# A two-layer encoder trunk on one core: from a planned order to the order of the text on every engine

## The chip, the core and the metric

The kernel runs on one core of a Trainium2 chip. TensorE (PE) multiplies; its weight loads (PEld) overlap its products. VectorE (DVE), ScalarE (ACT) and GpSimd (POOL) do the rest, SyncE (SP) issues most transfers. The metric is the device time of one execution in microseconds, median of the runs shown.

## The reference

The input is 256 tokens of 2048 features, and a memory of 256 tokens of 2048 features. Layer A normalises the tokens, multiplies by `a_w_in` (3584 columns), sends 1536 of them through a causal convolution and a gated linear recurrence (RG-LRU: sigmoid gates from 12 small products, then a scan over the tokens), gates the result by the GeLU of 1536 others, and lets the last 512 attend to the memory. Layer B has multi-head latent attention in place of the recurrence, and the same attention to the memory. Both layers end with `w_o` (2048 x 2048), a normalised residual, an MLP with squared ReLU (2048 to 8192 and back), and another normalised residual. Each layer makes memory keys and values from the normalised memory with weights of its own. All is float32.

## The kernel before, in words

Every weight block comes from DRAM as float32 and is split: ACT rounds it to float32r (`whi`, L108), DVE takes the rest (`wlo`, L109). `weights` (L116 to L131) loads 512 KB (two k-tiles of 512 columns) through SP's queue into one of five `wraw` buffers, and four `whi` and four `wlo` buffers hold what PE may use next. Activations are split in the same way into X tiles. `gemm` (L134 to L197) makes a block of columns: per k-tile and 128 outputs a 512-column and a 256-column product where features are wanted on partitions (L156, L157), or three products per 128 tokens where tokens are wanted on partitions (L166 to L168).

The order of each engine is planned: the framework simulates the program and issues by priority, with `tc.high_priority` around weight splits and evacuations. Work beside the products sits in generators (`bg`), a stage of which is traced after each group of k-tiles (`tick`), and the planner still moves it.

The stages in order, with the lines used below: memory values of layer A, whose X tiles grow from transposes of the memory (`to_features`, L231 to L252, transposes at L243); parameters (`rows`, L270 to L281, loaded through SP); tokens, their sums of squares (`stats`, L221) and transposes; memory keys; queries to the memory; three times a 512-column block of the recurrent branch and one of its gate (convolution L590 to L596, gates L599 to L606, recurrence L614 to L631 with a reciprocal at L623, GeLU L645 to L658, partly on POOL); `w_o` (`mix_out`); residual (`residual`, additions at L447); the MLP (8 blocks of two up and four down products); then layer B. The memory is transposed three times: once for layer A's keys and values, and once each for layer B's keys and values (`mem_features`, L528). The narrow last blocks of `PARTS` shorten the end of `mix_out` and of the MLP. The output leaves at L451.

Of the kernel before, what the change touches and what calls it, by code (L numbers as in the profile page):

```python
# [10 lines left out]
F32 = mybir.dt.float32  # L11
# [18 lines left out]
# columns of the output of a last block: narrow at the end, where the next phase waits for it  # L30
PARTS = [(0, 512), (512, 512), (1024, 512), (1536, 256), (1792, 256)]
SKEW = 1
# [15 lines left out]
def trunk(ctx: ExitStack, tc: tile.TileContext, a: dict, out: bass.AP):  # L48
# [16 lines left out]
    ctx.callback(phase.close)  # L65

# [1 line left out]
    # Work that fills the engines beside the products: generators, a stage of each running one per tick.  # L68
    # None in the queue: what follows waits for all before it.
# [3 lines left out]
    def tick():  # L73
# [7 lines left out]
        if bg:  # L81
            g = bg.popleft()
            if not next(g, True):
                active.append(g)
# [20 lines left out]
    def split(dst_hi, dst_lo, src, g=None):  # L105
        """dst_hi + dst_lo = src (times the column g), dst_hi rounded to float32r."""
# [9 lines left out]
    def weights(src, nk, n, gains=None):  # L116
        """[nk * 128, n] of DRAM, each row times its gain, as two float32r tiles [128, nk, n]."""
        raw = wp.tile([P, 1024], F32, name="wraw", tag="wraw", bufs=5)[:, : nk * n]
        nc.sync.dma_start(out=raw.rearrange("p (k n) -> p k n", k=nk), in_=src.rearrange("(k p) n -> p k n", p=P))
        hi = wp.tile([P, 1024], F32R, name="whi", tag="whi", bufs=4)[:, : nk * n]  # L120
        lo = wp.tile([P, 1024], F32R, name="wlo", tag="wlo", bufs=4)[:, : nk * n]
        with tc.high_priority(offset=200):
            if gains is None:
                split(hi, lo, raw)
            else:
                for k, g in enumerate(gains):
                    c = slice(k * n, (k + 1) * n)
                    split(hi[:, c], lo[:, c], raw[:, c], g)
        return hi.rearrange("p (k n) -> p k n", k=nk), lo.rearrange("p (k n) -> p k n", k=nk)
# [4 lines left out]
    def gemm(X, src, nk, n, bcols=(), a=None, evac_b=None, evac_a=None, kts=None, gain=None, pre=None, skew=0):  # L134
# [4 lines left out]
        kts = list(range(src.shape[0] // P)) if kts is None else kts  # L139
        groups = []  # L140
        for kt in kts:
            if groups and len(groups[-1]) < nk and groups[-1][-1] + 1 == kt:
                groups[-1].append(kt)
            else:
                groups.append([kt])
        W = {}
        psb = [mm.tile([P, 512], F32, name="psb", tag="mm") for _ in bcols]
        psa, one_bank = {}, False

        def by_features(i):  # L150
            ks, hi, lo = W[i]
            for j, b in enumerate(bcols):
                for k, kt in enumerate(ks):
                    Xk = X[kt // 4][:, kt % 4, :]
                    first, last = (i, k) == (0, 0), (i, k) == (len(groups) - 1, len(ks) - 1)
                    nc.tensor.matmul(psb[j], hi[:, k, b : b + P], Xk, start=first, stop=False)  # L156
                    nc.tensor.matmul(psb[j][:, 256:512], lo[:, k, b : b + P], Xk[:, 0:256], start=False, stop=last)  # L157

        def by_tokens(t, i):
            ks, hi, lo = W[i]  # L160
            for k, kt in enumerate(ks):
                Xk = X[kt // 4][:, kt % 4, :]
                xh, xl = Xk[:, t * P : (t + 1) * P], Xk[:, 256 + t * P : 256 + (t + 1) * P]
                first, last = (i, k) == (0, 0) and not (one_bank and t), (i, k) == (len(groups) - 1, len(ks) - 1)
# [4 lines left out]
                if last:  # L169
                    with tc.high_priority(offset=100):  # L170
                        evac_a(t, psa[t])

        for i, ks in enumerate(groups):
            if pre is not None:
                pre(ks[0])
            gains = gain and [gain(kt) for kt in ks]
            W[i] = (ks, *weights(src[ks[0] * P : (ks[-1] + 1) * P, :], len(ks), n, gains))
            if a is not None and i == 0:
                na = a(W[0][1][:, 0, :]).free_size()
                one_bank = na <= 256 and not skew  # L180
# [6 lines left out]
            if a is not None:  # L187
                by_tokens(0, i)
                if i >= skew:
                    by_tokens(1, i - skew)  # L190
            tick()
        if a is not None:
            for i in range(len(groups) - skew, len(groups)):
                by_tokens(1, i)
        with tc.high_priority(offset=100):
            for j in range(len(bcols)):
                evac_b(j, psb[j])  # L197
# [11 lines left out]
    def as_row(dst, r):  # L209
        """dst[p, token] = r of the token: [128, 256] from [128, 2]."""  # L210
# [12 lines left out]
    def rstd(dst, ss, n):  # L223
        """dst = (sum of ss over its last axis / n + EPS) ** -0.5, a column for every token block"""
# [6 lines left out]
    def to_features(chunk, nkt, gain, X, qs=None):  # L231
        """X (a list of X tiles) grows by the features of tokens, transposed, times gain(k), split.
        chunk(t, q): [128 tokens, up to 512 features] from feature 512 q."""
        for q in range(0, nkt, 4) if qs is None else [4 * q for q in qs]:
            kn = min(4, nkt - q)
            src = [chunk(t, q // 4) for t in range(NT)]
            X.append(xtile())
            for k0 in range(0, kn, 2):
                ps = aux()
                for k in range(k0, k0 + 2):  # L240
                    for t in range(NT):
                        c = (k - k0) * T + t * P
                        nc.tensor.transpose(ps[:, c : c + P], src[t][:, k * P : (k + 1) * P], ident)  # L243
                if gain is None:
                    split(X[-1][:, k0 : k0 + 2, 0:256], X[-1][:, k0 : k0 + 2, 256:512], ps.rearrange("p (k n) -> p k n", k=2))
                    continue
                for k in range(k0, k0 + 2):
                    c = (k - k0) * T
                    split(X[-1][:, k, 0:256], X[-1][:, k, 256:512], ps[:, c : c + T], gain(q + k))

    def scaled(src, r):
        """chunk() of tokens src [128, 2, n] scaled by the columns r."""  # L252

        def chunk(t, q):
            n = min(512, src.shape[2] - 512 * q)
            hn = scr(n, "hn")
# [635 lines left out]
```

## Time and profile before

| what | value |
|---|---|
| median of 3 runs | 2129.55 us (2128.59 to 2129.86) |
| profiled execution, first to last instruction (span) | 2126.1 us |
| PE busy | 2090.0 us, 98% |
| DVE, ACT, POOL busy | 1344.1, 1078.2, 99.1 us |
| DMA over the span | 394.98 MB, mean 186 GB/s |

The page gives the profiled execution its span; no total beside it is listed, and the median is 3.45 us more than the span. A busy PE is not PE at its peak, since matmul ends are modelled. Idle time of another engine costs only where PE waits for it.

### The profile page before, as it was taken

The page shows a single profiled execution, that of the slowest core. Times are in us where ns is not written, and L with a number is a line of the kernel's source. Part 1 is how long each engine was busy: PE and PEld are TensorE (multiplying, and loading weights), DVE is VectorE, ACT ScalarE, POOL GpSimd, SP SyncE. Part 2 cuts the span into 40 slices and gives each one's busy share as a digit, 9 for nine tenths or more (in the row PEclk, how much of TensorE's full clock was granted, in tenths as well). Part 3 has the DMA queues.
Part 4 walks back from the last instruction along what each step waited for, and adds up shares of the span by engine and source line. Part 5 has one row for each costly group of instructions (what it writes and reads, how often), then busy time and mean ns, then how long its engine had stood idle before and what let it go on. Part 6 is the DMA issues. An engine that isn't in the chain of part 4 may idle for free.

```text
span 2126.1 us, 29360 instructions
## 1 busy us (share of the span) xinstructions
PE 2090.0 (98%) x11167; PEld 1803.3 (85%) x11167; DVE 1344.1 (63%) x1923; ACT 1078.2 (51%) x1670; POOL 99.1 (5%) x141
## 2 busy tenths in 40 slices
PE   8999999999999999999999999989999999999997
PEld 7888779888888888888889898878888888888886
DVE  6678876664656656566576766566565656556565
ACT  7576655554444444445466655454543444434443
POOL 0023410000000000000010000000000000000001
PEclk9999999999999999999999999999999999999999
DMA  8555566656666566665656435655656566565663
GB/s 289 168 162 172 177 217 211 185 183 196 190 189 193 184 195 191 188 194 186 197 155 197 148 126 160 211 153 182 203 179 205 188 177 204 177 205 188 179 202 125
DMA packets 213121, 394.98 MB, mean 186 GB/s; under 512 B 12826, under 2 KB 36596, under 8 KB 212468
## 3 DMA queue, kind: packets, MB, share of 16 engines
q1 hardware_dynamic: 208964, 387.35, 58.9%
q10 hardware_dynamic: 4016, 5.77, 0.8%
q8 instruction: 87, 1.43, 0.3%
q14 instruction: 54, 0.44, 0.1%
HBM read 390.97 MB, written 2.10 MB: 185 GB/s over the span
## 4 chain that ended last, share of the span: by engine, by line
PE 82%; DVE 1%; issue 0%; ACT 0%; POOL 0%; DVEq 0%; POOLq 0%; ACTq 0%
PE psb L156 25%; PE psa L166 14%; PE psa L168 14%; PE psa L167 14%; PE psb L157 12%; PE aux L243 1%; PE aux L805 0%; PE aux L806 0%; DVE h L447 0%; PE aux L819 0%; PE aux L814 0%; PE aux L380 0%; PE aux L398 0%; PE aux L820 0%; PE aux L390 0%
## 5 line engine op out<-in xcount | busy, mean ns | idle before, releaser
L109 DVE TENSOR_TENSOR wlo<-wraw,whi 128x1024 fp32r<-128x1024 f32 (+1 forms) x694 | 847.0, 1228 | 666.7 <-ACT whi L108 662.3
L108 ACT CAST whi<-wraw 128x1024 fp32r<-128x1024 f32 (+1 forms) x694 | 720.8, 1046 | 817.8 <-PE psa L168 415.7
L156 PE MATMUL psb<-X,whi 128*128 128x512 f32 x2808 | 985.5, 399 | 3.3 <-DVE X L112 3.3
L157 PE MATMUL psb<-X,wlo 128*128 128x256 f32 x2808 | 763.0, 282 | 6.8 <-DVE wlo L109 6.8
L156 PEld LDWEIGHTS psb<-X,whi 128*128 128x128 f32 x2808 | 523.6, 189 | 117.2 <-DVE X L112 4.0
L167 PE MATMUL psa<-wlo,X 128*128 128x512 f32 (+3 forms) x1652 | 605.4, 367 | 3.5 <-DVE wlo L109 3.5
L166 PE MATMUL psa<-whi,X 128*128 128x512 f32 (+3 forms) x1652 | 601.4, 368 | 1.0 <-ACT whi L108 1.0
L168 PE MATMUL psa<-whi,X 128*128 128x512 f32 (+3 forms) x1652 | 602.1, 367 | 0.0
L157 PEld LDWEIGHTS psb<-X,wlo 128*128 128x128 f32 x2808 | 530.6, 189 | 20.5 <-DVE wlo L109 8.7
L167 PEld LDWEIGHTS psa<-wlo,X 128*128 128x128 f32 x1652 | 311.6, 189 | 52.5 <-DVE wlo L109 4.2
L166 PEld LDWEIGHTS psa<-whi,X 128*128 128x128 f32 x1652 | 311.0, 189 | 51.2 <-ACT whi L108 1.4
L168 PEld LDWEIGHTS psa<-whi,X 128*128 128x128 f32 x1652 | 310.9, 189 | 48.3
L501 DVE SCALAR_TENSOR_TENSOR y<-psa,r,y 128x512 f32<-128x512 f32 (+1 forms) x116 | 79.7, 726 | 7.0 <-PE psa L168 7.0
L506 POOL TENSOR_TENSOR y<-y,gpost 128x512 f32<-128x512 f32 x12 | 17.8, 1504 | 1399.6 <-ACT junk L221 723.4
L108 ACT CAST X<-ff 128x256 fp32r<-128x256 f32 x128 | 52.4, 410 | 57.8 <-DVE ff L484 57.8
L202 ACT COPY corr<-psb 128x256 f32<-128x256 f32 x192 | 69.7, 370 | 14.3 <-PE psb L157 11.9
L112 DVE SCALAR_TENSOR_TENSOR wlo<-wraw,pB,whi 128x384 fp32r<-128x384 f32 (+2 forms) x80 | 44.5, 599 | 22.7 <-ACT whi L111 22.5
L484 DVE SCALAR_TENSOR_TENSOR ff<-fs 128x256 f32<-128x256 f32 x128 | 54.2, 424 | 3.2
L111 ACT ACTIVATE whi<-wraw,pB 128x384 fp32r<-128x384 f32 (+2 forms) x80 | 43.6, 600 | 20.6 <-PE psa L168 19.3
L204 DVE TENSOR_TENSOR fs<-psb,corr 128x256 f32<-128x256 f32 x128 | 53.5, 418 | 0.6 <-ACT corr L202 0.6
L109 DVE TENSOR_TENSOR X<-ff,X 128x256 fp32r<-128x256 f32 x128 | 51.1, 419 | 4.3
L111 ACT ACTIVATE X<-aux,pB 128x256 fp32r<-128x256 f32 x48 | 21.4, 472 | 13.8 <-DVE X L112 8.8
(267 smaller groups left out, 797.2 us busy)
## 6 DMA issues: line engine op xcount, KB each, us to landing
wraw<-in_w_ff_dram SPq DMA_DIRECT2D x512, 512.0 KB, 4.2
wraw<-in_w_o_dram SPq DMA_DIRECT2D x64, 512.0 KB, 3.6
wraw<-in_a_w_in_dram SPq DMA_DIRECT2D x56, 512.0 KB, 4.2
wraw<-in_w_mem_v_dram SPq DMA_DIRECT2D x16, 512.0 KB, 4.5
wraw<-in_w_mem_k_dram SPq DMA_DIRECT2D x16, 512.0 KB, 3.6
wraw<-in_b_w_qb_dram SPq DMA_DIRECT2D x18, 384.0 KB, 3.5
mtok<-in_mem_dram SPq DMA_DIRECT2D x24, 256.0 KB, 7.3
wraw<-in_b_w_in_dram SPq DMA_DIRECT2D x16, 384.0 KB, 3.2
```

What stands on the lines that cost most here:

```text
L108: nc.scalar.copy(out=dst_hi, in_=src)
L109: nc.vector.tensor_tensor(out=dst_lo, in0=src, in1=dst_hi.bitcast(F32), op=ALU.subtract)
L111: nc.scalar.activation(dst_hi, src, AF.Copy, scale=g)
L156: nc.tensor.matmul(psb[j], hi[:, k, b : b + P], Xk, start=first, stop=False)
L157: nc.tensor.matmul(psb[j][:, 256:512], lo[:, k, b : b + P], Xk[:, 0:256], start=False, stop=last)
L166: nc.tensor.matmul(psa[t], xh, a(hi[:, k, :]), start=first, stop=False, **kw)
L167: nc.tensor.matmul(psa[t], xh, a(lo[:, k, :]), start=False, stop=False, **kw)
L168: nc.tensor.matmul(psa[t], xl, a(hi[:, k, :]), start=False, stop=last, **kw)
L202: nc.scalar.copy(out=c, in_=ps[:, 256:512])
L204: nc.vector.tensor_tensor(out=dst, in0=ps[:, 0:256], in1=c, op=ALU.add)
L484: nc.vector.scalar_tensor_tensor(out=f, in0=s, scalar=0.0, in1=s, op0=ALU.max, op1=ALU.mult)
L501: nc.vector.scalar_tensor_tensor(out=dst, in0=ps, scalar=r2[:, t : t + 1], in1=dst, op0=ALU.mult, op1=ALU.add)
```

## The change

`tc.manual_schedule()` is entered: every engine issues in the order of the text, and the priorities go. The weight blocks of the whole program are listed in one `stream`. `feed()` is traced ahead of each group: it splits up to `HELD` = 4 groups counted from the one in use, and loads up to `RAW` = 5 beyond the last split one. Other work is cut into more stages. Evacuations of feature blocks come right behind the last product of each 128 outputs.

```
+    def feed(hold=0):
+        while True:
+            if n_split < min(n_used + HELD - hold, n_loaded):
+                convert()
+            elif n_loaded < min(n_split + RAW, len(stream)):
+                load()
             else:
+                return
...
         for i, ks in enumerate(groups):
+            feed()
             if pre is not None:
                 pre(ks[0])
...
             tick()
+            if after is not None:
+                after(i)
+        if halves is not None:
+            for i in range(len(groups)):
                 by_tokens(1, i)
+                n_used += 1
+                halves(i)
```

The memory's gain moves into the weights of keys and values, so that one set of memory features serves both layers: it is transposed once, written to DRAM (`mem_x`) and reloaded for layer B through POOL's queue. The start is written out by hand (`fetch` loads 2 x 256 KB of memory through SP, `mem_turn` transposes them, `mem_sums` takes sums on ACT):

```
+    def after(i):
+        if i == 0:
+            fetch(2)
+        elif i in (2, 4):
+            mem_turn(i // 2 + 1)
+            mem_sums(i // 2 + 1)
+            if i == 2:
+                fetch(3)
+                params.extend(other_rows())
...
+    fetch(0)
+    load()
+    load()
+    mem_turn(0)
+    convert()
+    convert()
+    fetch(1)
+    load()
+    load()
+    mem_sums(0)
+    mem_turn(1)
+    mem_sums(1)
+    mem_values(0, XM, after=after)
...
+    for _ in stats(rh[0], h):
+        pass
+    bg.extend(features(XA, h, rh[0], g_mix[0]))
     mem_keys(0, XM)
```

The 10 parameter loads of `other_rows` move from SP's queue to ACT's (`nc.scalar.dma_start`), and the transposes of what they load follow them directly. Loads of `gpost`, the gate weights and the positions move from ACT's queue to POOL's.

In the recurrence the reciprocal and two scalings go; an exponential on ACT and two DVE multiplications come, and one stage `root` now holds four exponentials and a square root on ACT. The convolution's fourth tap moves from ACT and POOL to DVE, and the GeLU's last subtraction from POOL to DVE, so that POOL has 12 in place of 24 multiplications or additions per block of 512 columns. The queries to the memory come behind the recurrence.

Layer B's `w_o` and its MLP end by halves: in the last block the first 128 tokens' products are all issued ahead of the second's, and while the second's run the first's residual is made, either transposed at once or stored:

```
+        def evac(self, t, y, ss):
+            self.y = y
+            rstd(self.r[:, t : t + 1], ss[:, t, :], D)
+            if t == 1:
+                self.turn(0, 3)
+                add(y, self.r, 1, 0)
+                self.turn(1, 0, lambda: add(y, self.r, 1, 1))
...
+        def after(self, i):
+            if i == 0:
+                self.X.extend(xtile() for _ in range(4))
+                feed()
                 for q in range(4):
+                    add(self.y, self.r, 0, q)
+            elif i == 1:
+                feed()
+                self.turn(0, 0)
+            elif i == 2:
+                feed()
+                self.turn(0, 1)
+                self.turn(0, 2)
```

`add` is one addition of 128 x 512 (as L447), `turn` four transposes and their splits of 128 columns. The remaining three quarters of the second half's features are added and transposed one per two groups behind the first up products (`rest`). Layer B's last MLP block has four parts of 512 columns in place of `PARTS`.

## Rows read from the trace of the kernel before

**Rows 1.** The page's first line and its busy times.
```profile
span 2126.1 us, 29360 instructions
PE 2090.0 (98%) x11167; PEld 1803.3 (85%) x11167; DVE 1344.1 (63%) x1923; ACT 1078.2 (51%) x1670; POOL 99.1 (5%) x141
```

**Rows 2.** Stretches: length, busy us of each engine (count), granted clock, DMA share, GB/s.
```profile
150.00:175.00 25.00, 22.74 (x122) 19.54 (x121) 23.79 (x33) 13.55 (x24) 13.20 (x12) 0.93 0.55 163
...
200.00:225.00 25.00, 20.47 (x113) 16.79 (x112) 21.89 (x28) 16.43 (x26) 13.90 (x15) 1.00 0.52 149
...
250.00:275.00 25.00, 22.04 (x104) 18.03 (x103) 21.85 (x29) 17.80 (x31) 15.27 (x16) 1.00 0.54 161
...
800.00:850.00 50.00, 50.00 (x246) 42.20 (x246) 30.47 (x38) 22.94 (x29) 0.00 (x0) 1.00 0.60 191
```

**Rows 3.** Waits of PE in the recurrence, 125 to 290: us in total, times, longest.
```profile
PE psb L157 <- DVE wlo L109: 6.8, 5, 3.2
```

**Rows 4.** Timeline of PE inside an MLP block: start, us.
```profile
816.26 0.39 PE L156 MATMUL psb<-X,whi 128*128 128x512 f32 x1
...
816.61 0.40 PE L156 MATMUL psb<-X,whi 128*128 128x512 f32 x1
```

**Rows 5.** The chain that ended last, in order of time: start, us.
```profile
387.03 0.87 PE aux L243 x8
...
1404.68 0.43 PE psb L156
1405.32 0.43 PE psb L156
```

**Rows 6.** Groups by line and shape, PE: the memory's transposes.
```profile
L243 PE MATMUL aux<-ident,mtok 128*128 128x128 f32 x96 | 15.9, 287 | 3.1 <-DMA mtok<-in_mem_dram 3.1
```

**Rows 7.** Groups by line and shape, DVE, then ACT, in the recurrence, 125 to 285.
```profile
L109 DVE TENSOR_TENSOR wlo<-wraw,whi 128x1024 fp32r<-128x1024 f32 x47 | 60.9, 1305 | 14.6 <-ACT whi L108 14.5
L623 DVE RECIPROCAL rec<-av 128x256 f32<-128x256 f32 x12 | 20.9, 1740 | 0.0
L653 DVE SCALAR_TENSOR_TENSOR gs<-gs,ga 128x256 f32<-128x256 f32 x12 | 9.8, 817 | 0.1
...
L614 ACT ACT_TABLE_LOAD x3 | 3.8, 1283 | 0.1
```

**Rows 8.** The page's groups: a two-input DVE operation in the MLP.
```profile
L484 DVE SCALAR_TENSOR_TENSOR ff<-fs 128x256 f32<-128x256 f32 x128 | 54.2, 424 | 3.2
```

**Rows 9.** Timeline of the start: start, us, engine and line.
```profile
9.56 1.22 PE L166 MATMUL psa<-whi,X 128*128 128x512 f32 x2 [1.01 <-ACT whi L108]
...
28.81 0.63 ACT L221 ACTIVATE junk<-mtok 128x512 f32<-128x512 f32 x1
...
30.73 0.46 SPq L276 DMA_DIRECT2D pB_st<-in_g_mix_pre_dram  x1
```

**Rows 10.** DMA issues: queue, count, KB each, median us to landing.
```profile
wraw<-in_w_ff_dram SPq DMA_DIRECT2D x512, 512.0 KB, 4.2
...
out_dram<-h SPq DMA_DIRECT2D x8, 256.0 KB, 2.5
```

**Rows 11.** Timeline between layer B's `w_o` and its MLP.
```profile
1393.04 0.28 PE L167 MATMUL psa<-wlo,X 128*128 128x256 f32 x1
1393.15 0.28 PE L168 MATMUL psa<-whi,X 128*128 128x256 f32 x1
...
1397.19 5.39 DVE L447 SCALAR_TENSOR_TENSOR h<-y,ry,h 128x512 f32<-128x512 f32 x8 [0.81 <-POOL ry L229]
...
1403.04 0.80 PE L156 MATMUL psb<-X,whi 128*128 128x512 f32 x1 [1.98 <-DVE X L112]
```

**Rows 12.** Timeline of the end.
```profile
2115.02 0.28 PE L168 MATMUL psa<-whi,X 128*128 128x256 f32 x1
...
2115.74 2.73 DVE L447 SCALAR_TENSOR_TENSOR h<-y,ry,h 128x512 f32<-128x512 f32 x4
...
2118.39 0.42 DVE L506 TENSOR_TENSOR y<-y,gpost 128x256 f32<-128x256 f32 x1
```

More of the change, by code (lines that the diff above doesn't have):

```diff
@@ L81, in tick @@
         if bg:
-            g = bg.popleft()
-            if not next(g, True):
-                active.append(g)
+            item = bg.popleft()
+            for g in item if isinstance(item, tuple) else (item,):
+                if not next(g, True):
+                    active.append(g)
     def flush():
@@ L114, in split, with __init__ @@
             )
[L116 to L124, printed above, removed]
-            else:
[L126 to L129, printed above, removed]
+    class Gemm:
+        def __init__(self, src, nk, n, kts=None, gain=None, single=0):
+            self.src, self.nk, self.n, self.gain, self.groups, self.W = src, nk, n, gain, [], {}
+            for kt in range(src.shape[0] // P) if kts is None else kts:
+                last = self.groups[-1] if self.groups else None
+                if last and len(last) < nk and last[-1] + 1 == kt and len(self.groups) > single:
+                    last.append(kt)
+                else:
+                    self.groups.append([kt])
+            stream.extend((self, i) for i in range(len(self.groups)))
@@ L131, in xtile, with gemm @@
+    def feed(hold=0):
[4 more added lines that the diff above has]
+                load()
+            else:
+                return
     def xtile():
         return xp.tile([P, 4, 512], F32R, name="X", tag="X")
[L134 to L146, printed above, removed]
+    def gemm(G, X, bcols=(), a=None, evac_b=None, evac_a=None, pre=None, after=None, halves=None):
+        nonlocal n_used
+        assert stream[n_used] == (G, 0)
+        groups = G.groups
@@ new lines, in turn, with features, one @@
+            if k0 + 2 < kn:
+                yield
+    def features(X, src, r, gain):
+        n = src.shape[2]
+        def one(q):
+            c = slice(512 * q, min(n, 512 * (q + 1)))
+            hn = [scr(c.stop - c.start, "hn") for _ in range(NT)]
+            for t in range(NT):
+                nc.vector.tensor_scalar_mul(hn[t], src[:, t, c], r[:, t : t + 1])
+            yield
+            X.append(xtile())
+            yield from turn(X, q, hn, gain)
+        return [one(q) for q in range((n + 511) // 512)]
@@ L423, in mix_out @@
             c = slice(n0, n0 + n)
+            last = halves is not None and q == len(PARTS) - 1
             def ev(t, ps):
@@ new lines, in ev, with add @@
+                if q == 0:
+                    bg.append(times_gain())
+                else:
+                    next(times_gain(), None)
+                if last:
+                    halves.evac(t, got[0], ss)
+            gemm(WO[l][q], X, a=lambda w: w, evac_a=ev, pre=pre, halves=halves.after if last else None)
+        return got[0], ss, got[2]
+    def add(y, r, t, q):
+        c = slice(512 * q, 512 * (q + 1))
+        nc.vector.scalar_tensor_tensor(
+            out=h[:, t, c], in0=y[:, t, c], scalar=r[:, t : t + 1], in1=h[:, t, c], op0=ALU.mult, op1=ALU.add
+        )
@@ new lines, in trunk, with __init__, evac, leave @@
+    class Ended:
+        def __init__(self):
+            self.r = small(NT, "ry")
+        def evac(self, t, y, ss):
+            self.y = y
+            rstd(self.r[:, t : t + 1], ss[:, t, :], D)
+            if t == 1:
+                self.leave(1)
+        def leave(self, t):
+            for q in range(4):
+                add(self.y, self.r, t, q)
+                c = slice(512 * q, 512 * (q + 1))
+                (nc.sync if q % 2 == 0 else nc.scalar).dma_start(out=out_t[:, t, c], in_=h[:, t, c])
+        def after(self, i):
+            if i == 0:
+                self.leave(0)
@@ new lines, in trunk, with fetch @@
+    WQ.append(Gemm(wb[:, QR : QR + 512], 2, 512, gain=gain_of("mix1")))
+    WQB, WKV = [], []
+    for g in range(3):
+        WQB.append(Gemm(a["b_w_qb"][0][:, 768 * g : 768 * (g + 1)], 1, 768))
+        WKV.append([Gemm(a["kv_w_up"][:, n0 : n0 + 512], 2, 512) for n0 in (1024 * g, 1024 * g + 512)])
+    plan_out(1, [*range(12, 16), *range(12)])
+    plan_mlp(1, False)
+    lp = enter("lru", 2)
+    XM, XA = [], []
+    ssm = sums(4, "ss")
+    chunks = {}
+    def fetch(q):
+        chunks[q] = [scr(512, "mtok") for _ in range(NT)]
+        for t in range(NT):
+            nc.sync.dma_start(out=chunks[q][t], in_=mem_t[:, t, 512 * q : 512 * (q + 1)])
@@ L595, in conv @@
                     )
-                nc.gpsimd.tensor_tensor(out=xc, in0=xc, in1=tap, op=ALU.add)
                 yield
```

505 lines of the change are left out of this document (292 added, 213 removed).

## The prediction

> **What bounds the kernel now.** The page's busy times come first: PE is busy for 2090.0 of 2126.1 us and every other engine is far below [rows 1]. The reader should see that at most 36 us can come from PE's stops, and that the rest must be fewer or faster products. The table of stretches says where the stops are: inside the MLP (800 to 850) PE is busy for all of 50 us, while three stretches of 25 us in the recurrence lack 2.26, 4.53 and 2.96 us, together 9.75 [rows 2]. PE's waits name their cause there: products with `wlo` wait for DVE's split, five times and up to 3.2 us [rows 3], while DVE is busy for 21.9 to 23.8 us of each 25 [rows 2]. The pace inside the MLP is 0.35 us from one 512-column product of a pair to the next [rows 4], and the change reorders nothing within a group of k-tiles, so that I cost the products that stay at nothing.
>
> After a stop PE also runs slowly: behind the stop at 1403 the pairs are 0.64 us apart in place of 0.35 [rows 5, 4], TensorE at 1.2 GHz, the lower of its two levels, in place of 2.4. In the stretch with the stop of 2.26 us the mean granted clock is 0.93 [rows 2]: between the levels 1 and 0.5 that is 0.07 x 25 / 0.5 = 3.5 us at half speed, so 1.75 us lost besides the stop. I use 1.75 for each stop of over 2 us.
>
> The sum is made against the profiled span, 2126.1; the median of the runs is 3.45 us above it, which I add at the end.
>
> **Memory transposed once.** 96 transposes become 32 [rows 6]. Eight take 0.87 us [rows 5], so 64 x 0.11 = **7.0 us less** on PE, which is on the path since PE has no gaps where they stand. Neither bound is far. What replaces them, 4 MB written and 8 MB read, is taken at nothing: at 191 GB/s [rows 2] the queues have room. If the reloads come late there is a rival, below.
>
> **The recurrence.** The three stops and their slow clock cost 9.75 + 3 x 1.75 = 15 us. The edit removes the reciprocals, 20.9 us of DVE or 7.0 per block of 512 columns [rows 7], and adds 12 two-input operations per block: the third tap on DVE, the second multiplication, the GeLU's subtraction, four each. One costs 0.42 us undisturbed [rows 8] and 0.82 beside POOL [rows 7], so 5.1 to 9.8 us: DVE itself gets between 1.9 us lighter and 2.8 heavier per block. POOL's operations halve, which moves prices towards the lower end. So DVE stays close to full, and the gain is mainly that splits are now issued at a fixed lead of three groups, 3 x 8 pairs x 0.35 = 8.4 us. `root` eats into that lead: two table loads at 1.28 us [rows 7] and five calculations hold ACT, and every split queued behind it, for some 5 us. Bounds: 0 (all stays) and 15; I take **12 us less**, nearer the upper, because the lead outlasts that hold.
>
> **The start.** Here the order of the text costs. Three waits replace what the planner interleaved; the first product stays where it is, near 9.6 [rows 9], since it needs the same transfers.
> (a) `fetch(2)` stands on SP behind five weight loads, the last of which waits until the fourth block is split. That split is on ACT behind four sums at 0.75 (0.63 and its readout, [rows 9]), four splits of transposes and an earlier block: about 17 to 18 us. Landing takes 2.5 us for 256 KB where little else is under way, 4.2 for 512 KB in the MLP [rows 10]; PE reaches the transposes at about 18. 0 to 4.5; taken 2.
> (b) Behind them PE's next instructions are the transposes of the parameters. Their ten loads are issued by ACT, after its splits and sums of those same transposes: 0.7, then 10 x about 0.4 [rows 9], then 2.5 to land [rows 10]: 7 us in which PE has nothing else that it may issue. If ACT must first end its four operations, 9.5; if the loads were issued ahead, 0. Taken 7.
> (c) The sums of squares of the tokens are eight in a row on ACT behind the last product of the values, 6 us, then 1.5 for the rest, then scaling. PE has two groups, 5.6 us, before the transposes that need them: 1 to 5, taken 3.
> Together **12 us more** (1 to 19).
>
> **Between layer B's `w_o` and its MLP.** Before, PE stops from 1393.3 to 1403.0 [rows 11], less twelve transposes at 0.11. In the change only two additions and a few splits follow the last product, about 4 us of chain: 4 us better if DVE is free by then. But in the second half, 4 groups of 12 products 0.12 us apart [rows 11] or 5.8 us, the text gives DVE three weight splits at 1.3 [rows 7], four additions at 5.39 / 8 = 0.67, and twelve splits of 128 columns, which no row shows (half of 0.42 to all of it [rows 8]): 9.1 to 11.6 us. The last evacuation is queued behind these, 3 to 6 us late, and `rest` adds three waits of about 1. Bounds -4 to +4.5; I take **1.5 us more**.
>
> **The end.** The first tokens' four additions, 2.73 us, now stand between the last product and the last multiplication of the second tokens, which starts only at 2118.39 [rows 12]. By halves they run during the second half's products. Minus 2.5, plus 0.5 for a last block of 512 columns: **2.0 us less** (1 to 3).
>
> **The rest.** Layer A's two transitions to and from its MLP bring additions, transposes and splits of weights with gains into the same groups, and layer B's attention brings more stages per group; both have waits before and after. Taken at 0; bounds, estimated from one split of 1.3 us [rows 7] more or less in each of some six places, -2 and +8. What hides them is the lead of 8.4 us; without it each late split is PE's wait.
>
> Sum: -7.0 - 12 - 2.0 + 1.5 + 12 + 0 = -7.5, a span of 2118.6, and with 3.45 **2122 us**.
>
> **Rivals.**
> *The start decides (slower).* All three waits come at their upper ends, 4.5 + 9.5 + 5, each with its slow clock, 3 x 1.75: 24.3 in place of 12, so **2134.5**. For it: in the order of the text SP, ACT and PE issue nothing past a waiting instruction, and each wait hands on to the next. Against: landing is quick on an idle queue. It decides from 24 us on, where slower by over 0.2% begins.
> *DVE stays the bound of the recurrence.* DVE was at 87 to 95% there [rows 2] and in order it also waits for ACT and POOL. Then the 12 us don't come: **2134**.
> *All waits hidden.* The start costs 4, the transition gains 3, 8 + 4.5 less: **2109.5**. For it: PE's reach is my estimate, and `w_o`'s second half may free DVE.
> *Reloads late.* Reloads of memory features go out from POOL, 1 MB each; at 4.2 us per 512 KB [rows 10] one takes 8.4, against 5.5 us of products per tile. Not issued ahead, a pass loses up to 8.4 + 3 x 2.9 = 17. Before, POOL sat idle 95% of the time [rows 1], so mostly they go out ahead; a loss of 10 gives **2132**. The Trainium skill ("SBUF — State Buffer", SBUF: two separate sides) warns of this: a transfer issued from GpSimd needs descriptors that it writes itself, and certain VectorE operations lock it out of the port it needs. By that rule the reloads would wait for DVE's operations and the time would be this rival's; no row here shows a transfer from POOL.
> *The order is not what it says* (the planner's order happens to be that of the text) would leave the MLP as it is and all else near 2120; it has no chance of its own.
>
> **How the numbers follow.** 0.2% (4.3 us) is about what a measurement of this kernel can tell from no change: faster lies below 2125.3, slower above 2133.8. My sum has 0.40: most of its spread (2113 to 2131, terms half way to their bounds) is faster, 0.28, and 0.12 within. All hidden 0.18, faster. The start 0.20, slower. DVE's bound 0.12: 0.08 slower, 0.04 within. Late reloads 0.10: 0.07 within, 0.03 slower. Faster 0.46, same 0.23, slower 0.31. Both signs carry weight, so the range is wide: from 2104 (all hidden, with the other terms at their good bounds) to 2144 (start and recurrence both bad).
>
> **What would show it.** Memory transposes 32 in number. In 150 to 275 no stretch lacking over 1 us of PE; if DVE is named again, the second rival. PE's waits list `pA_st` or `pB_st` with some 7 us, `mtok` with 2 and `hn` with 3; three times that or none tells start and hidden apart. A stop of 7 to 11 us before layer B's MLP, with DVE splits in it. About 8.5 us from last product to end, 10.8 now. The MLP's blocks at the same pace; if they are not, the whole argument is wrong, since 1400 us lie there.

## The result, and the profile after

The changed kernel takes 2283.3 us (2281.9 to 2286.7, 4 runs) against 2129.2 us before: 1.073 times as long, 95% interval 1.071 to 1.074. Faster was forecast, 2122. First the head of the changed kernel's page:

```profile
span 2279.8 us, 29088 instructions
PE 2132.8 (94%) x11055; PEld 1820.4 (80%) x11055; DVE 1322.6 (58%) x1954; ACT 1075.5 (47%) x1665; POOL 70.6 (3%) x129
```

and its core's mean granted clock:

```profile
core 0: 2279.8 us, clock 0.972
```

PE's idle time is 2279.8 - 2132.8 = 147.0 us, 36.1 before [rows 1]: 110.9 more. PE is also *busy* 42.8 us longer, though it turns 64 tiles less: a mean clock of 0.972 means (1 - 0.972) / 0.5 x 2279.8 = 128 us at the lower level, 1.2 GHz, of which half, 64 us, is lost; before (0.994) it was 13. So 111 us of new stops, 51 us of slow clock behind them, 7 us of transposes saved: 155, where the spans differ by 153.7.

Next, the four stretches of [rows 2] in the changed kernel (length, busy us of each engine, clock, DMA share, GB/s).

```profile
150.00:175.00 25.00, 23.62 (x120) 20.30 (x121) 17.03 (x29) 10.63 (x18) 4.70 (x7) 0.87 0.46 133
200.00:225.00 25.00, 17.92 (x91) 14.97 (x90) 13.81 (x22) 14.04 (x23) 6.79 (x9) 0.86 0.39 122
250.00:275.00 25.00, 22.91 (x118) 18.93 (x117) 9.60 (x16) 15.59 (x27) 2.94 (x4) 0.96 0.28 84
800.00:850.00 50.00, 50.00 (x245) 42.09 (x244) 30.93 (x41) 23.28 (x30) 0.00 (x0) 1.00 0.63 194
```

The MLP keeps its pace. In the recurrence PE lacks up to 7 us of 25, and DVE is now busy for 9.6 to 17.0 us there, not 22 to 24. No engine is the bound; they wait for each other.

The stages, each from the start of the last product of one block to that of the next, of the kernel before, the changed one and five experiments (us):

| stage | before | changed | e4 | e12 | e18 | e15 | e17 |
|---|---|---|---|---|---|---|---|
| start: values, keys A | 62.3 | 87.3 | 89.6 | 76.6 | 78.2 | 68.7 | 67.4 |
| recurrence, query A | 186.6 | 221.7 | 199.0 | 181.7 | 181.5 | 199.2 | 170.3 |
| `w_o` A | 95.8 | 105.7 | 99.8 | 100.9 | 101.3 | 104.1 | 102.1 |
| keys B | 25.8 | 39.0 | 38.1 | 26.1 | 26.1 | 24.5 | 24.5 |
| MLP A | 713.5 | 722.4 | 723.5 | 722.6 | 711.6 | 710.2 | 710.2 |
| values B | 23.8 | 32.6 | 34.0 | 25.4 | 25.4 | 21.9 | 21.9 |
| projections, query B | 87.2 | 86.6 | 85.1 | 84.5 | 84.5 | 86.5 | 86.5 |
| attention B | 100.3 | 134.0 | 118.9 | 120.5 | 109.8 | 101.5 | 101.4 |
| `w_o` B | 97.8 | 103.1 | 100.6 | 100.6 | 100.6 | 97.3 | 97.3 |
| MLP B | 721.9 | 736.3 | 733.2 | 728.5 | 728.8 | 723.6 | 723.4 |
| last product to end | 11.1 | 11.1 | 11.0 | 11.5 | 11.5 | 12.3 | 12.3 |

Almost every transition has lost; the largest are the recurrence, the attention and the start. The same stretches of the changed kernel, for the five worst:

```profile
0.00:53.61 53.61, 33.37 (x134) 26.27 (x135) 22.27 (x38) 25.86 (x48) 4.33 (x13) 0.84 0.80 293
...
87.30:309.01 221.71, 184.38 (x945) 153.97 (x944) 133.10 (x244) 118.79 (x192) 34.64 (x45) 0.92 0.45 137
...
414.73:453.73 39.00, 30.05 (x162) 25.48 (x161) 21.85 (x38) 15.44 (x30) 4.55 (x38) 0.87 0.59 201
...
1295.28:1429.29 134.01, 110.32 (x673) 98.69 (x672) 76.01 (x176) 61.83 (x143) 0.00 (x0) 0.92 0.35 106
...
1532.43:2268.76 736.33, 719.43 (x3606) 607.79 (x3605) 428.27 (x547) 331.95 (x452) 9.97 (x10) 0.99 0.59 180
```

PE's waits, in total, times, longest:

```profile
PE psb L199 <- DVE ga L250: 20.2, 3, 6.7
PE psa L211 <- DVE rw L995: 18.9, 3, 6.7
PE aux L535 <- DVE h L496: 12.0, 2, 10.3
PE aux L286 <- DMA mtok<-in_mem_dram: 8.5, 3, 6.5
PE psb L200 <- DVE wlo L115: 7.8, 10, 3.1
PE aux L329 <- DMA pB_st<-in_kv_g_in_dram: 6.2, 1, 6.2
PE psb L199 <- DMA X<-mem_x: 6.1, 1, 6.1
...
PE psa L211 <- DMA X<-mem_x: 5.3, 1, 5.3
PE aux L286 <- DVE hn L305: 4.8, 3, 3.6
```

The two longest are not waits for weights, as in [rows 3]: `ga` (L250) and `rw` (L995) are DVE's last reads of a PSUM bank, and PE waits for the bank. Three times each, once in each of the loop's three rounds. How one comes about, on ACT, then DVE, then PE:

```profile
132.72 1.28 ACT L835 ACT_TABLE_LOAD   x1
...
137.02 1.06 ACT L836 ACTIVATE st<-th 128x1024 f32<-128x1024 f32 x1
137.99 1.03 ACT L114 CAST whi<-wraw 128x1024 fp32r<-128x1024 f32 x1
140.71 0.42 ACT L849 ACTIVATE th<-th 128x256 f32<-128x256 f32 x1 [1.69 <-DVE th L843]
141.07 1.05 ACT L114 CAST whi<-wraw 128x1024 fp32r<-128x1024 f32 x1
144.33 0.42 ACT L849 ACTIVATE th<-th 128x256 f32<-128x256 f32 x1 [2.21 <-DVE th L843]
144.65 1.03 ACT L114 CAST whi<-wraw 128x1024 fp32r<-128x1024 f32 x1
...
149.15 0.64 ACT L248 COPY corr<-psb 128x256 f32<-128x256 f32 x2
...
139.06 1.23 DVE L115 TENSOR_TENSOR wlo<-wraw,whi 128x1024 fp32r<-128x1024 f32 x1 [7.74 <-ACT whi L114]
140.20 0.42 DVE L843 SCALAR_TENSOR_TENSOR th<-av,th 128x256 f32<-128x256 f32 x1
...
142.15 1.23 DVE L115 TENSOR_TENSOR wlo<-wraw,whi 128x1024 fp32r<-128x1024 f32 x1 [1.20 <-ACT whi L114]
143.30 0.68 DVE L852 TENSOR_TENSOR_SCAN xi<-th,st 128x256 f32<-128x256 f32 x1
...
150.42 0.75 DVE L250 TENSOR_TENSOR ga<-psb,corr 128x256 f32<-128x256 f32 x2
...
150.89 0.79 PE L199 MATMUL psb<-X,whi 128*128 128x512 f32 x1 [6.72 <-DVE ga L250]
```

Read it as a ring. ACT copies weights (L114); DVE, which has nothing else that it may issue, waits for that copy and subtracts (L115); then come DVE's steps of the recurrence (L852, L843), on which ACT's next step (L849) waits; only then may ACT copy the next weights. One turn is 144.33 - 140.71 = 3.6 us, where PE needs 8 x 0.35 = 2.8 us per group. `root` has opened the lag: its tables and calculations hold ACT from 132.72 to 138.08, 5.4 of the 7.74 us that DVE stands idle before 139.06. The evacuation (L248, L250) is queued behind all of this, and PE, its weights split, has no free bank: 6.72 us. The product after the stop takes 0.79 us, the lower clock. Over the whole recurrence (87.30 to 309.01) DVE waits for ACT's copies of weights 34 times, 63.1 us:

```profile
DVE wlo L115 <- ACT whi L114: 63.1, 34, 7.7
```

### The profile page after: what moved, and what is told of

It is laid out like the page before. It is cut to its first block, busy times and chain, and to the rows that moved or that the text cites. A ratio compares the mean times of both kernels' runs of the same rounds, so it can differ in the third digit from the quotient of the medians.

```text
span 2279.8 us, 29088 instructions
## 1 busy us (share of the span) xinstructions
PE 2132.8 (94%) x11055; PEld 1820.4 (80%) x11055; DVE 1322.6 (58%) x1954; ACT 1075.5 (47%) x1665; POOL 70.6 (3%) x129
## 4 chain that ended last, share of the span: by engine, by line
PE 79%; DVE 9%; ACT 7%; issue 3%; DMA 1%; POOL 0%; ACTq 0%; SPq 0%; DVEq 0%; POOLq 0%
PE psb L199 23%; PE psa L211 14%; PE psa L213 14%; PE psa L212 14%; PE psb L200 12%; DVE wlo L115 3%; ACT whi L114 2%; DVE wlo L118 1%; ACT junk L267 1%; DVE X L118 1%; DMA X<-mem_x 1%; ACT X L117 1%; DVE xc L813 1%; DMA mtok<-in_mem_dram 1%; PE aux L286 1%
## 5 line engine op out<-in xcount | busy, mean ns | idle before, releaser
L115 DVE TENSOR_TENSOR wlo<-wraw,whi 128x1024 fp32r<-128x1024 f32 x662 | 805.5, 1224 | 760.4 <-ACT whi L114 760.4
L199 PE MATMUL psb<-X,whi 128*128 128x512 f32 x2808 | 1022.0, 407 | 40.0 <-DVE ga L250 20.2
L114 ACT CAST whi<-wraw 128x1024 fp32r<-128x1024 f32 x662 | 686.3, 1043 | 574.4 <-PE psa L213 329.0
L200 PE MATMUL psb<-X,wlo 128*128 128x256 f32 x2808 | 798.5, 284 | 7.8 <-DVE wlo L115 7.8
L199 PEld LDWEIGHTS psb<-X,whi 128*128 128x128 f32 x2808 | 538.6, 192 | 173.9 <-DVE ga L250 21.1
L617 ACT CAST X<-fs 128x256 fp32r<-128x256 f32 x128 | 52.0, 407 | 214.7 <-DVE fs L616 214.7
L248 ACT COPY corr<-psb 128x256 f32<-128x256 f32 x192 | 68.3, 371 | 54.9 <-DVE fs L250 26.6
L619 DVE TENSOR_TENSOR X<-fs,X 128x256 fp32r<-128x256 f32 x128 | 53.5, 418 | 0.0
L616 DVE SCALAR_TENSOR_TENSOR fs<-fs 128x256 f32<-128x256 f32 x128 | 53.4, 417 | 0.0
L118 DVE SCALAR_TENSOR_TENSOR wlo<-wraw,pM,whi 128x512 fp32r<-128x512 f32 x64 | 45.0, 747 | 13.7 <-ACT whi L117 13.4
L117 ACT ACTIVATE whi<-wraw,pM 128x512 fp32r<-128x512 f32 x64 | 42.2, 714 | 22.6 <-PE psa L213 15.1
L250 DVE TENSOR_TENSOR fs<-psb,corr 128x256 f32<-128x256 f32 x128 | 48.1, 418 | 5.2 <-ACT corr L248 5.2
```

The lines of the kernel that those rows point to most:

```text
L114: nc.scalar.copy(out=dst_hi, in_=src)
L115: nc.vector.tensor_tensor(out=dst_lo, in0=src, in1=dst_hi.bitcast(F32), op=ALU.subtract)
L117: nc.scalar.activation(dst_hi, src, AF.Copy, scale=g)
L118: nc.vector.scalar_tensor_tensor(out=dst_lo, in0=src, scalar=g, in1=dst_hi.bitcast(F32), op0=ALU.mult, op1=ALU.subtract)
L248: nc.scalar.copy(out=c, in_=ps[:, 256:512])
L619: nc.vector.tensor_tensor(out=F[:, j, 256:512], in0=s, in1=F[:, j, 0:256].bitcast(F32), op=ALU.subtract)
```

## The experiments

T1, my theory, is that ACT and DVE form such rings, and that the evacuations that free PSUM stand behind them; the later theories (T3 to T12) are named in the expectations. Its rivals are the other edits (R1) and the lead of weights (R2). Effects below are on the changed kernel's 2283.3 unless another is named; where one run was made, its profile's stages carry the reading.

**e1: the planner on the changed text** (the line `ctx.enter_context(tc.manual_schedule())` deleted).

> The changed kernel with its order written by the planner again; all other edits stay. T1 (the order of the text is the cause: ACT and DVE wait for each other in turn, and the evacuations that free PSUM stand behind them): 2115 to 2150 us, the products of the recurrence and of layer B's attention back near 187 and 100 us (222 and 134 in the changed kernel). R1 (the other edits are the cause: operations moved to DVE, reloads and parameters issued from POOL and ACT): stays above 2230.

Measured 2161.5 us (ratio to before 1.014, 1.013 to 1.016): the attention is back at 100.9, the recurrence only at 198.8. Order costs 122 us, but some 30 are left, more than the 2115 to 2150 expected.

**e2: five split groups held** (`HELD = 5`, `RAW = 3`).

> Five split weight groups held in place of four (three raw ones in place of five, to fit). R2 (the lead of weights is too short for what holds ACT): the stops of 6.7 us in the recurrence and the attention shrink below 4 us each, 2240 to 2260 in all. T1: PE stops there with weights ready and no free PSUM bank, so they stay at 6 to 7 us: 2275 to 2295.

2302.9 us, above both ranges; the longest stops at `ga` are 7.6 and at `rw` 6.7 us. A longer lead of split weights takes nothing off, and R2 falls. (Only three raw buffers fit beside it, and MLP A takes 729.8 us: the edit has a cost of its own.)

**e4: the two halves of a weight split a group apart.**

```
-            split(hi, lo, raw)
+            parts = [(hi, lo, raw, None)]
...
+        if owed:
+            low()
+        for p in parts:
+            split(*p, part=0)
+        owed.append(((G, i), parts))
...
+    def low():
+        for p in owed.pop()[1]:
+            split(*p, part=1)
```

(`part=0` is ACT's copy, `part=1` DVE's subtraction, which `low` issues for the group before.)

> DVE's half of each weight split is issued one group later than ACT's half, so that DVE never waits for the copy that ACT is just about to make; nothing else changes. T1: the ring ACT copy, DVE subtraction, DVE stage, ACT stage is cut, a tick costs the larger of the two engines' work and not their sum: the three stops in the recurrence fall from 6.7 to below 4 us, the three in the attention to below 3, 2200 to 2245 in all. R1 and R2: nothing changes or, with one group less lead on DVE's side, some us more: 2280 to 2300.

2233.3 us (ratio to before 1.048, 1.047 to 1.050), 50 us less with the same operations. Recurrence and attention in e4, and DVE's waits for ACT's copies in the recurrence:

```profile
89.55:288.50 198.95, 177.28 (x945) 150.92 (x944) 138.81 (x248) 122.12 (x196) 41.63 (x45) 0.96 0.52 161
...
1269.04:1387.95 118.91, 106.08 (x673) 96.12 (x672) 76.17 (x176) 61.72 (x142) 0.00 (x0) 0.97 0.39 120
...
DVE wlo L118 <- ACT whi L115: 7.1, 7, 1.9
```

Against the changed kernel 23 and 15 us are gone, the clock is at 0.96 and 0.97 in place of 0.92, and DVE waits for ACT's copies for 7.1 us in place of 63.1. The longest stops are 2.6 us at `ga` and 3.6 at `rw` (below 4 and below 3 were expected). T1 holds.

**e5: `1 - th` on POOL** (L849 as a `tensor_scalar` of POOL).

> In the recurrence 1 - th is computed by POOL in place of ACT, so that ACT's next copy of weights no longer waits for DVE's operation of the stage. T1: the loop of 3.6 us per tick falls to about DVE's own 2.8, the stops of 6.7 us at L250 in the recurrence to 3 to 4: 10 to 16 us less, 2267 to 2275. R1 (DVE's load is what counts): DVE has the same work, no change within 3 us.

2280.0 us: 3 less, not 10 to 16; the longest stop at `ga` is 5.4 us. The same place in e5, on ACT, POOL and DVE:

```profile
142.06 3.88 ACT L114 CAST whi<-wraw 128x1024 fp32r<-128x1024 f32 x4
...
145.26 1.70 POOL L850 TENSOR_TENSOR st<-st,xi 128x256 f32<-128x256 f32 x1
...
146.99 0.69 DVE L852 TENSOR_TENSOR_SCAN xi<-th,st 128x256 f32<-128x256 f32 x1 [0.64 <-POOL st L850]
```

ACT is out of the ring and copies four groups of weights in a row, but POOL has taken its place: its multiplication (L850) takes 1.70 us, 0.74 in the changed kernel, DVE's scan waits for it, and from one L843 to the next it is still 3.3 us (147.60 to 150.90). So e5 exchanged one ring for another and doesn't tell what a turn of 2.8 would give. The lag that `root` opens stays: by an estimate from the trace above, three turns 0.8 us above PE's 2.8 make 2.4 of the 6.7 us.

**e6: the reloads issued together** (all four at `kt == 0` of their product, not one at every fourth k-tile).

> The changed kernel with all four reloads of memory features issued at the first group of their product, in place of one at every fourth k-tile. T3 (the reloads are late because on POOL they stand behind an operation that waits for VectorE): the two waits for a reload, 6.1 and 5.3 us, vanish with the half-speed stretches behind them, K1 and V1 together 14 to 20 us shorter than in the changed kernel, 2264 to 2270. R3 (the transfers themselves are slow, 8 to 14 us each, whoever issues them): the waits shrink by less than half.

2268.2 us, both waits gone, keys and values B shorter by 9.0 and 7.2: T3. In the changed kernel POOL did this:

```profile
417.95 0.72 POOL L275 TENSOR_TENSOR ry<-var,neghalf 128x2 f32<-128x2 f32 x1 [108.51 <-DVE var L274]
418.63 1.64 POOL L668 DMA_DIRECT2D X<-mem_x  x3
```

Three reloads, 0.55 us each to issue, stood behind POOL's power in `rstd`, which waited for the sum of a product still running. The transfers themselves are no faster in e6 (from issue to landing 11.2 us in the median of eight, 9.0 in the changed kernel); they only start in time.

**e7: parameters loaded at the top, turned at the sixth group; memory's chunks fetched one place earlier.**

```
+    other = other_rows()
...
-            fetch(2)
+            fetch(3)
...
-                fetch(3)
-                params.extend(other_rows())
...
         elif i == 5:
             rstd(rmem, ssm, D)
+            params.extend(f() for f in other)
...
+    fetch(2)
     mem_values(0, XM, after=after)
```

> The loads of the parameters are issued by ACT at the very top and turned only at the sixth group of the values' product; the memory's third and fourth chunks are fetched one place earlier on SP, ahead of the weight loads that wait for a buffer. T4 (the start's loss is the order of the issues): the waits for mtok (8.5 us) and for pB and pA (7.4 us) fall below 3 us together, V0 from 53.6 to 38 to 42 us, 2267 to 2273. Rival: PE is held there by the splits of the first weights, and the time comes back as waits for whi or wlo: V0 above 47.

2273.5 us; the first product block ends 9.4 us earlier (44.2), the waits for `pB` and `pA` are gone and `mtok`'s are 4.6 us. T4, though short of its 38 to 42 for that block and its 3 us for the waits.

**e8: in a tile's splits ACT's parts first, then DVE's** (`for part in range(2): for k in range(4)`, in `Mixed.turn` and in `turn` with a gain).

> Between w_o and the MLP (and wherever a gain is split in pieces) ACT makes its parts of a tile one after the other and DVE follows with its parts, in place of one pair after the other. T5 (in pairs each half waits for the other engine's, 0.78 us per 128 columns, and so the last evacuation comes late): four pairs take about 1.7 to 2.4 in place of 3.1 us, the stop of 10.35 us before layer B's MLP falls to 5 to 8, 4 to 8 us less in all, 2275 to 2280. Rival: the evacuation is held by the weight splits and additions ahead of it, whatever the pairs do: the stop stays above 9.5.

2271.6 us, 12 less, more than the 4 to 8 expected; the longest wait before MLP B is 4.8 us, MLP B 7.9 shorter. In the changed kernel (ACT, then DVE):

```profile
1538.72 0.37 ACT L117 ACTIVATE X<-aux,pB 128x128 fp32r<-128x128 f32 x1 [0.42 <-DVE X L118]
1539.51 0.37 ACT L117 ACTIVATE X<-aux,pB 128x128 fp32r<-128x128 f32 x1 [0.42 <-DVE X L118]
...
1539.12 0.35 DVE L118 SCALAR_TENSOR_TENSOR X<-aux,pB,X 128x128 fp32r<-128x128 f32 x1 [0.43 <-ACT X L117]
1539.91 0.35 DVE L118 SCALAR_TENSOR_TENSOR X<-aux,pB,X 128x128 fp32r<-128x128 f32 x1 [0.43 <-ACT X L117]
```

ACT's part waits even for DVE's part of *another* k-tile, so a pair costs 0.79 us. In e8:

```profile
1528.61 2.17 ACT L118 ACTIVATE X<-aux,pB 128x128 fp32r<-128x128 f32 x8
...
1530.68 2.16 DVE L121 SCALAR_TENSOR_TENSOR X<-aux,pB,X 128x128 fp32r<-128x128 f32 x8
```

Eight in 2.17 us on each engine, 0.27 apiece. Both parts read one PSUM bank. The Trainium skill ("PSUM — Partial Sum Buffer", PSUM bank collisions raise a hardware error) says that two engines must not touch one bank at once, reads included, and are kept apart by semaphores; the alternation above agrees, though no run separates it from a dependency through the tile `X`.

**e9: the planner with the old priorities** (`high_priority` around splits and evacuations, which the changed text dropped).

> The changed text under the planner, with the priorities of the kernel before given back (200 for the splits of weights, 100 for evacuations), which the changed text had dropped. T1 (order is the whole loss; the 30 us that the planner still lost on the changed text came from the missing priorities): 2115 to 2135. Rival (the edits themselves, later heads, more operations on DVE, reloads from POOL, cost those 30 us): 2150 to 2165.

2163.8 us (ratio to before 1.015 to 1.018), no less than e1: the rival came true. The 30 us lie in the edits.

**e10, e11: on e4, `root` spread over three groups** (a `yield` after two Exp and after four, `bg.append(None)` behind) **and the newest stage issued first** (in `tick`, the new item begins before the active ones go on).

> On top of e4_skew: the four Exp and the Sqrt of the recurrence's step `root` are issued over three groups in place of one. T6 (what is left in the recurrence after e4_skew is the hold of some 5 us that root puts on ACT, with the weight copies queued behind it): the stops on wlo and ga behind it fall, the products of the recurrence from 199.0 to 188 to 194 us, 2223 to 2229 in all. Rival: the stage itself, now two groups longer, costs the same at the end of the block: 2231 to 2237.

> On top of e4_skew: in every group the newest stage of the work beside the products is issued ahead of the older ones. T7 (what is left in the attention is a second ring, ACT exponentials, ACT copy for the output, DVE subtraction, DVE maximum of the next head, ACT exponentials, 4.65 us a turn): the maximum no longer stands behind the subtraction that waits for ACT, the three stops of 3.6 us at rw fall below 1.5 each, the attention's products from 118.9 to 105 to 112 us, 2220 to 2228. Rival (the evacuations stand behind the last weight splits, not behind the ring): the stops stay at 3 to 4 us, 2230 to 2236.

e10: 2227.0 us, recurrence 189.6, as T6 said. e11: 2222.5 us, but not by T7: the attention stays at 120.4 with stops of 3.2 us, as its rival said, and the gain is in the recurrence, 189.7, which I had not expected.

**e12: e4 to e8, e10 and e11 together.**

> All edits that answered, together: e4_skew, e5_thpool, e6_reload, e7_start, e8_order, e10_root, e11_new. If the losses are separate places as T1 and T3 to T7 say, the gains add: 50 + 3 + 14 + 8 + 11 + 8 + 9 = 103 us, 2175 to 2190. If one stop only moves to the next place, less than 75 of them come: above 2208. None of the theories expects the kernel before (2129) to be reached, since the hold of root, the transitions and rest's waits remain in part.

2179.4 us (ratio to before 1.023, 1.022 to 1.025). The single gains are 50 + 3 + 15 + 10 + 12 + 6 + 11 = 107 us, together they give 104: separate places. The recurrence takes 181.7 us, before 186.6, but some 6 us of its head products have moved on to `w_o` A (PE busy for 97.9 us there, before 92.2, both at clock 1.00): the two stages together take 282.6 us, 282.4 before.

**b1: the kernel before with one transposition less** (features for keys B written out, read back for values B).

> The kernel before, whose memory features for layer B's keys are also written to DRAM and read back for layer B's values, in place of a second transposition. Nothing else changes. The term of the sum alone (32 transposes at 0.11 us on PE, no stop added): 3.5 us less, ratio 0.998 to 0.999. Rival (a reload issued in its place comes late, as 5.3 to 6.1 us waits in the changed kernel): no gain or up to 5 us more, ratio 1.000 to 1.003.

2126.1 us against 2129.9, ratio 0.9983 (0.9974 to 0.9992): the 3.5 us of 32 transposes, and no late reload. Faster than either kernel, by 0.2% of the kernel before.

**e13, e14: on e12, the last group's weight split behind the evacuation; rope from SBUF after a copy by ACT.**

> On top of e12_all: in the last group of every product the next weight split is issued behind the evacuations in place of ahead of them. T8 (the stops of 3.2 us at rw in the attention come from evacuations that stand behind one last weight split of 1.2 us on each engine): the stops fall by 1 to 1.5 us each, the attention's products from 120.5 to 114 to 117 us, 2170 to 2176 in all. Rival (it is the length of the evacuation itself, four additions and two turns by rope on DVE, some 5 us): the stops stay, and the later splits cost some us elsewhere: 2177 to 2185.

> On top of e12_all: in the attention the query's rotary part is evacuated by one copy on ACT per half, and the four DVE operations of the rotation run from SBUF in the stage that follows. T9 (rope on DVE is what holds the PSUM bank): the waits for rw, 9.3 us, vanish or pass to another evacuation at under 1.5 us each, the attention's products from 120.5 to 106 to 112 us, 2164 to 2172 in all. Rival (T8, the evacuations stand behind splits): a wait of 2.5 to 3.2 us stays under another name, 2176 to 2182.

e13: 2180.2 us. The waits at `rw` fall from 9.3 to 5.9 us and the attention to 112.3, more than T8 said, but `wlo` waits grow from 10.8 to 18.5 us elsewhere, and the total is in the rival's range. e14: 2171.2 us, in T9's range, but the attention is 114.6, not 106 to 112; of 9.3 us 6.8 stay, now for ACT's copy.

**e16: on e14, the rotation's tables spread over MLP A's first groups** (`rope_tables` a generator handed to `mlp` as `first`).

> e14_rope, and the tables of the rotation, 8 us of small DVE operations in one piece ahead of layer A's MLP, are spread over the first groups of that MLP, where DVE is idle for half of the time. T11 (the stop of 6.2 us at wlo ahead of the MLP is that piece, with the weight splits behind it): MLP0 from 722.6 to 714 to 717 us, 6 to 9 us below e14_rope. Rival (the stop is due to the residual's additions and splits, which run there too): below 3 us less than e14_rope.

2162.8 us, 8 less than e14, MLP A 713.3 in place of 720.7: T11.

**e18: on e16, e13's order in the attention alone.**

> e16_tables, with the next weight split issued behind the evacuations in the attention's products alone (e13_evf did so in all). T8 and T9 together (both the rotation and the splits stand ahead of the evacuations): the waits for qraw, 6.8 us, fall below 4, the attention's products from 113.1 to 106 to 110 us, and nothing is lost elsewhere: 2154 to 2161. Rival (e13_evf gained there and e14_rope gained there by the same few us): 2161 to 2165.

2159.3 us (ratio to before 1.013, 1.012 to 1.015), attention 109.8, wait for the copy 3.3 us, as expected. Two causes, both in part.

**e15, e17: which edits cost under the planner.** e15 is e9 with e6, e8 and e10; e17 has the recurrence of the kernel before in place of the Exp (`reciprocal` on DVE, `root` the Sqrt alone).

> e9_prio (the changed text under the planner, with priorities) plus the edits of e6_reload, e8_order and e10_root, to see which of the other edits cost the 30 us that order doesn't explain. T10 (they are the Exp and Sqrt of root, 12 us, the late reloads, some 11, the pairs of splits): 2133 to 2145. Rival (they lie in what the edits add to the engines all over): 2155 to 2165.

> e15_planfix (the changed text under the planner) with the recurrence computed as in the kernel before: the reciprocal on DVE and its operations on ACT back, no Exp in root, no av of four. T12 (under the planner too, the edit of the recurrence costs, because root now holds ACT for two tables and five calculations while the weight copies wait): the recurrence's products from 199.2 to 186 to 191 us, 2139 to 2144 in all. Rival (the planner loses there for another reason, the late heads or the third tap on DVE): 197 or more, 2149 to 2155.

e15: 2151.9 us, above T10's 2133 to 2145: 12 us less than e9, from keys and values B (24.5 and 21.9, in e9 32.8 and 29.9), and the recurrence unchanged at 199.2. e17: **2119.7 us**, one run, where the lowest of seven runs of the kernel before beside it was 2128.1; recurrence 170.3, with `w_o` A 272.5, 9.9 less than before. T12 had expected 2139 to 2144 and 186 to 191. The recurrence's stretch, and the table loads on ACT, of e15:

```profile
68.72:267.94 199.22, 175.88 (x945) 151.06 (x944) 132.05 (x218) 137.99 (x207) 37.41 (x77) 0.93 0.48 151
```

```profile
L828 ACT ACT_TABLE_LOAD x9 | 11.5, 1283 | 0.2
L842 ACT ACT_TABLE_LOAD x9 | 11.5, 1283 | 0.2
```

The same two views of e17:

```profile
67.40:237.73 170.33, 168.63 (x946) 145.74 (x944) 139.80 (x211) 113.30 (x189) 33.83 (x40) 1.00 0.55 172
```

```profile
L828 ACT ACT_TABLE_LOAD x3 | 3.8, 1283 | 0.1
L840 ACT ACT_TABLE_LOAD x3 | 3.8, 1283 | 0.1
```

T12, and more than I had named: in e15 the planner alternates Sigmoid (L828) and Exp (L842), and each turn loads a table; with Sqrt and GeLU, three each, these are 24 loads. The order of the text groups them, 12; e17, without the Exp, has 9 (its L840 is the Sqrt). PE's waits for weight splits in the recurrence are 23.4 us in e15 and 4.2 in e17. With this edit taken back (and e10's spreading with it) the planner gains 32 us. How much of that is the loads is not shown: 15 fewer at 1.283 are 19 us of ACT, but the calculations changed with them, and no run keeps the Exp and groups its loads under the planner. How the old recurrence fares in the order of the text was not tried either.

## Why the prediction was wrong

**Memory transposed once: right.** 32 transposes stand in the trace, and b1 finds 3.8 us (1.7 to 5.5) for half of the term. Its cover was not: "they go out ahead" failed. The rival with late reloads had the waits, 6.1 and 5.3 us, and a fair price for a transfer (8.4 us, 9.0 measured in the median), but not the reason: e6 leaves the reloads on POOL, and the waits vanish. It was POOL's order, so nothing here shows an effect of the rule on GpSimd's descriptors (the Trainium skill, "SBUF — State Buffer", SBUF: two separate sides).

**The recurrence: the step that failed.** -12 forecast, +35.1 measured, and +45.0 with `w_o` A, into which head products moved (327.4 us for both, before 282.4). DVE got lighter, as reckoned. What failed is "splits are now issued at a fixed lead of three groups" and "the lead outlasts that hold". The lead covers a late *split*. A late *evacuation* has only one spare bank of five, a quarter of a group's 2.8 us or 0.7, and in order it stands behind the same lag; e2 shows that the lead is not what lacks. I also summed each engine's load by itself; a ring costs the sum of the operations chained on both engines, 3.6 us a turn (1.03 and 0.42 on ACT, 1.23, 0.68 and 0.40 on DVE, less small overlaps), where DVE alone has 2.7 (with L846's 0.42). e4 and the later edits take all of it back, to 282.6 for both stages, but none in the order of the text shows the 12 us of gain. The one run that shows some (e17, 9.9) has the planner's order and the old arithmetic, so it came another way than the forecast said.

**"The rest" at 0, -2 to +8: the largest error.** It is +69 us: keys B 13.2, MLP A 8.9, values B 8.8 (in keys and values stand the late reloads, 16 us by e6), attention 33.7, `w_o` B 5.3, the projections -0.6. The sentence "What hides them is the lead of 8.4 us" was wrong in the same way. The attention has such a ring through its softmax: its exponentials on ACT wait for DVE's maximum (12 times, 33.5 us), DVE's subtractions for ACT's copies (26 times, 43.8 us, in e4 3 times, 5.5 us). MLP A begins behind 8 us of small operations that make the rotation's tables (e16); in the kernel before they run during `w_o` A.

**The start.** +12 forecast, +25.0 measured. (b), 7 us, came as 7.4; (c), 3, as 4.8; (a), 2 (at most 4.5), was 8.5, of which waits for `mtok` had 3.1 before. `fetch(2)` went out at 16.28, even earlier than reckoned, but landed 7.2 us later: I had priced it at 2.5, from the output's stores, when the kernel before has a row for these very loads:

```profile
mtok<-in_mem_dram SPq DMA_DIRECT2D x24, 256.0 KB, 7.3
```

The slow clock, which I had left out of that sum, costs another 8.6 us (0.84 over the first 53.6 us). The rival's 24.3 us is near what happened, partly by luck: its (a) was too small, its (b) too large, and it left the rest of the kernel as forecast. (Its time should read 2134.3.)

**Between `w_o` B and its MLP.** The stop and the transposes take 14.6 us (1532.43 to 1547.02), 9.9 before [rows 11]: +4.7, just past the bound of 4.5, where I took 1.5. The mis-sized term is the split of 128 columns: 0.79 us a pair on two engines that wait in turn, not 0.21 to 0.42. With `rest`'s waits and the clock MLP B is 14.5 us longer.

**The end.** -2.0 forecast, -0.05 measured. The additions did move under the products, but a block of 512 columns has longer operations (0.74, 0.63 and 0.69 us, where the kernel before had 0.48, 0.42 and 0.42), and the span ended 4.3 us after the last transfer's issue, 3.6 before.

**The clock.** I priced 1.75 us for a stop of over 2 us. In the recurrence the mean clock of 0.92 over 221.7 us is 17.7 us lost, behind 37 us of stops. Stops and slow clock come nearly two to one over the whole kernel, 111 to 51.

None of my cases reached beyond 2144, since each took one or two places at a time and let the others be hidden.

## What to carry to other kernels

When a planner's order is replaced by that of the text, the engines' loads say little: follow, for each group, who waits for whom, and look for a ring between two engines and for what stands ahead of the evacuation. Issue the half of a pair that waits one group after the half that it waits for, releases of PSUM ahead of work for later groups, and loads ahead of any operation that waits. Taking one engine out of a ring is not enough if another steps in (e5). And time an edit of the arithmetic apart from an edit of the order: here what was left without one edit of either kind, and with two repairs (e17, one run), was some 10 us faster than the kernel before.

## What was not expected of the hardware

A table load on ACT takes 1.283 us in every case here, and how many there are depends on the order: 24 loads in the planner's recurrence (e1, e9, e15) and 12 in the text's, for the same functions. ACT and DVE, in pairs over 128 columns of one PSUM bank, take 0.79 us a pair; in runs of eight, 0.27 us each.

Left open: in e18 the attention still needs 9.5 us more than before, and the start 16; no run took these apart. e17 was run once.
